# Weight-block loads of the projection jobs, and the stores of their split halves, issued from ScalarE's DMA queue instead of SyncE's

## The chip, the cores and the metric

One core of one Trainium2 chip runs the whole program. The metric is device time in microseconds (us), the median of several executions.

## What is computed

One layer of a streaming encoder over 2048 prompt rows and 32 sample rows of width 1024, all in float32. What matters here, from the reference:

```
z = h @ w_in                                  # 1024 x 10256: q, k, v, gates, ...
o, s_new = gated_delta_chunked(q, k, v, ...)  # per head, 64-frame blocks, a serial state S
merged = sigmoid(..) * (y_a @ w_proj_a) + sigmoid(..) * (y_b @ w_proj_b)
h1 = layer_norm(ALPHA * h + merged @ w_out, ...)
ple = sigmoid(h1 @ w_ple_gate) * (p @ w_ple)
h2 = layer_norm(ALPHA * h1 + ple, ...)
```

Every large product is made in three passes: each matrix is split into a rounded high part and a low part (the rest), and high*high, high*low and low*high are added up.

## The kernel before

The rows are worked in two halves (`HALVES`): half 0 has 1024 prompt rows and the 32 sample rows, half 1 the other 1024 prompt rows. A half goes through three stages: the projection jobs of `w_in` ("wz", 80 blocks of 128 output columns) with the gated delta rule woven in between; the merge (`merge`), jobs with the branch matrices "wb" and "wa" (8 blocks each) and the last gates of "wz"; and the row stages `out_rows` and `ple_rows` (through `rows`), with "wo" and "wg", whose pieces are the moving operand.

**A weight block.** `load_w` (L229) brings one block of 128 x 1024 into two tiles, `wh` (high) and `wl` (low), which have two buffers each. In half 0 a block is met for the first time: the raw block is loaded into `wr` (two buffers, L247), ScalarE rounds it into `wh` (L248), VectorE (or GpSimd, in the row stages) subtracts to get `wl` (L249), and both parts are stored to DRAM (L251) for later. When the same block is needed again, its two parts are loaded directly (L243). All of these transfers, and every other one of the kernel, are issued by SyncE (SP, "SPq" in the rows).

**Jobs.** A `Job` (L254) is one weight block times all columns of the half: 3 groups of 352 columns in half 0, 2 groups of 512 in half 1, 24 matmuls per group (L273), then an evacuation of the accumulator by ScalarE or VectorE. `run` (L280) calls `load` for the next job before it writes out the groups of the current one. Between the matmuls `fill.pump()` takes steps of the delta rule: its preparation (`delta_prep`, with small transfers at L600, L641, L645, L656, L659) and its state loop (`delta_loop`, L758 to L786), which pass through TensorE, VectorE and ScalarE in turn.

**Row stages.** `rows` (L979) loads a piece (L998, L1004) and multiplies it with the row tiles (L988 to L991). `out_rows` loads `lnx` tiles (L1043) and stores them (L1055), `ple_rows` loads them and `pw` tiles (L1064, L1081).

**Order.** The program is written in one sequence; the tile framework orders the instructions of each engine by priority, among those whose inputs and buffers it expects to be there. On the chip each engine and each queue takes its own instructions in that fixed order.

Of the kernel before, what the change touches and what calls it, by code (L numbers as in the profile page):

```python
# [8 lines left out]
F32 = mybir.dt.float32  # L9
# [84 lines left out]
def hybrid_kernel(ctx: ExitStack, tc: tile.TileContext, I, O):  # L94
    nc = tc.nc
    ve, ac, po, pe = nc.vector, nc.scalar, nc.gpsimd, nc.tensor
# [129 lines left out]
                ac.copy(out=oh, in_=p[:, :, :n])  # L226
                ve.tensor_tensor(out=lo[:, 4 * b:4 * b + 4, l0:l0 + n], in0=p[:, :, :n], in1=oh.bitcast(F32), op=ALU.subtract)

    def load_w(name, at, low, into=None):  # L229


        src, kept = I[name], split_d[name]
        for i in at:
            src, kept = src[i], kept[i]

        def cut(x):
            return x.rearrange("p (a b) -> p a b", a=2) if into else x

        parts = into or [wp.tile([128, 1024], F32R, tag=x, name=x) for x in ("wh", "wl")]
        hi, lo = parts  # L240
        if (name, at) in stored:
            for i, t in enumerate(parts):
                nc.sync.dma_start(out=t.bitcast(F32), in_=cut(kept[i]))  # L243
            return parts
        stored.add((name, at))
        raw = cut(wp.tile([128, HP + NS], F32, tag="wr", name="wr")[:, :1024])
        nc.sync.dma_start(out=raw, in_=cut(src))  # L247
        ac.copy(out=hi, in_=raw)  # L248
        low.tensor_tensor(out=lo, in0=raw, in1=hi.bitcast(F32), op=ALU.subtract)  # L249
        for i, t in enumerate(parts):  # L250
            nc.sync.dma_start(out=cut(kept[i]), in_=t.bitcast(F32))  # L251
        return parts

    class Job:  # L254
# [6 lines left out]

        def load(self):
            if self.w is None:
                self.w = load_w(self.src[0], self.src[1:], ve)

        def group(self, g0, n):
            rh, rl = self.x or (xh, xl)
# [12 lines left out]
    def run(jobs, first=0, back=False, between=None):  # L280


        with tc.high_priority(1500):
            for j in jobs[:first]:
                if j.open:
                    j.open()
                j.load()
        for i, g in enumerate(jobs[0].groups[::-1] if back else jobs[0].groups):
            for j in jobs[:first]:
                j.group(*g)  # L290
            if i == 0 and between:
                between()
        for j in jobs[:first]:
            if j.close:
                j.close()
        jobs = jobs[first:]
        for i, j in enumerate(jobs):
            if j.open:
                j.open()
            j.load()  # L300
            if i + 1 < len(jobs):
                jobs[i + 1].load()
            for g in j.groups:
                j.group(*g)
            if j.close:
                j.close()


    def phase0(hf, lp, g, b, batches):
# [83 lines left out]
    def beta_decay(hf, gp):  # L393
# [90 lines left out]

        job = Job(None, hf.groups, None, close)
        job.load, job.group = load, group
        return job, out

# [420 lines left out]
    def merge(hf, mp):  # L909
# [54 lines left out]
        for c in range(KT):  # L964
            wa[c].open = lambda c=c: load_gate(c)
        run(gb_ + wb + late + wa)
        for g in hf.ogroups:
            for k in range(KT):
# [6 lines left out]
    def hold(q):  # L975

        load_w("wg", (1, q), po, [t[:, 2 * q:2 * q + 2, 512:HP] for t in (xh, xl)])

    def rows(src, npiece, kh, kl, cols, done, after=None, last=1):  # L979
# [17 lines left out]
        for q in range(npiece - last):  # L997
            w = load_w(*src(q), po)  # L998
            for kk in range(2):
                for a, (t0, n) in zip(accs, cols):  # L1000
                    step(a, t0, n, 2 * q + kk, *w, halves[kk])
            if after:
                after(q)
# [132 lines left out]
    for hf in HALVES:  # L1136
        with pool(f"gp{hf.idx}") as gp:
# [15 lines left out]
            for h in range(H + hf.sample):  # L1153
                cols = Cols(sc[h == H], slice(0, 8) if h == H else slice(8 * h, 8 * h + 8))
                u, t, g = Us[h % 2], ts[h], smp_got if h == H else got[h]
# [10 lines left out]
            jobs += bj + [gate_a_job(hf, c, gp) for c in range(KT)]  # L1166
            fill.rate = [0.275, 0.56] if hf.sample else [0.41, 0.82]
            run(jobs, 3, *((True, lambda: deque(reload, 0)) if hf.idx else ()))
            fill.drain()
        early.close()  # L1170
# [103 lines left out]
```

## Time and profile before

| | us |
|---|---|
| median of 3 runs | 3216.71 (3216.45 to 3217.76) |
| the profiled execution, its own time | 3223.0 |
| its span, first to last instruction | 3221.3 |
| TensorE (PE) busy | 3065.1 (95%) |
| VectorE (DVE) busy | 1911.1 (59%) |
| ScalarE (ACT) busy | 887.2 (28%) |

Busy times are sums over one execution. DMA-issuing instructions are not counted as busy, so ScalarE's and SyncE's shares do not hold what a transfer costs its issuer. A wait line names who waited, for whom, the sum in us, the number of waits and the longest.

### The profile page before, as it was taken

To read this page: it belongs to the slowest core of one execution; us is meant where nothing else is said; L and a number is where in the kernel's file an instruction comes from. 1 tells how busy PE (TensorE), PEld (TensorE's weight loads), DVE (VectorE), ACT (ScalarE), POOL (GpSimd) and SP (SyncE) were. 2 spreads that over 40 slices of the span, in tenths; PEclk is the share of its full clock that TensorE was granted. 3 is DMA by queue.
4 is the path that set the end of the run, shared out by engine and by line. 5 is a ranking of instruction groups with operands and counts; after the bars stand their busy time and mean duration, and the time that the engine had idled before them with its cause. 6 is when DMAs were issued, how large, how long until landed. Compare 5 with 4: busy or idle time off the path is not lost.

```text
span 3221.3 us, 51399 instructions
## 1 busy us (share of the span) xinstructions
PE 3065.1 (95%) x20524; PEld 2679.5 (83%) x20524; DVE 1911.1 (59%) x4759; ACT 887.2 (28%) x2152; POOL 225.4 (7%) x349
## 2 busy tenths in 40 slices
PE   7999999999999999999989999999999999999997
PEld 5998899999999999997767877778877788888776
DVE  6866887777877422343656568777677730123366
ACT  3333443343333221221212223333233211111010
POOL 2110000100000000002221000000000000000001
PEclk8999999999999999999989999999999999999999
DMA  7643233333333454557773322232322234444685
GB/s 281 230 151 110 91 125 115 122 121 119 117 110 121 150 199 166 181 187 256 277 259 131 119 90 84 82 96 84 96 90 85 84 110 145 158 131 133 227 299 189
DMA packets 176416, 477.07 MB, mean 148 GB/s; under 512 B 54640, under 2 KB 59280, under 8 KB 175792
## 3 DMA queue, kind: packets, MB, share of 16 engines
q1 hardware_dynamic: 176176, 473.78, 42.7%
q8 instruction: 161, 2.64, 0.3%
q14 instruction: 79, 0.65, 0.1%
HBM read 293.29 MB, written 180.41 MB: 147 GB/s over the span
## 4 chain that ended last, share of the span: by engine, by line
PE 68%; DVE 18%; issue 8%; DMA 3%; POOL 1%; ACT 1%; SPq 0%; DVEq 0%; POOLq 0%; ACTq 0%
PE acc L273 56%; DVE ktm L559 4%; DVE vtm L559 3%; DVE at L559 1%; DVE v L523 1%; PE oo L768 1%; PE sc L777 1%; PE oo L778 1%; PE sc L766 1%; POOL sg L1088 1%; PE sc L758 1%; DVE dt L609 1%; PE pp L686 1%; PE pp L629 1%; DVE lnx L206 1%
## 5 line engine op out<-in xcount | busy, mean ns | idle before, releaser
L273 PE MATMUL acc<-xh,wl 128*128 128x352 f32 (+1 forms) x3200 | 718.0, 361 | 0.0
L273 PE MATMUL acc<-xh,wh 128*128 128x352 f32 (+1 forms) x3200 | 714.5, 359 | 0.7 <-ACT xh L226 0.7
L273 PE MATMUL acc<-xl,wh 128*128 128x352 f32 (+1 forms) x3200 | 711.3, 359 | 0.0
L273 PEld LDWEIGHTS acc<-xh,wl 128*128 128x128 f32 x3200 | 553.7, 190 | 54.4 <-issue 1.6
L273 PEld LDWEIGHTS acc<-xh,wh 128*128 128x128 f32 x3200 | 552.0, 190 | 55.3 <-issue 1.4
L273 PEld LDWEIGHTS acc<-xl,wh 128*128 128x128 f32 x3200 | 551.6, 190 | 53.1 <-issue 1.8
L248 ACT CAST wh<-wr 128x1024 fp32r<-128x1024 f32 x112 | 117.3, 1048 | 266.3 <-PE acc L273 197.8
L249 DVE TENSOR_TENSOR wl<-wr,wh 128x1024 fp32r<-128x1024 f32 x96 | 117.2, 1221 | 73.6 <-PE acc L273 43.7
L919 DVE TENSOR_TENSOR yl<-yr,yh 128x1056 fp32r<-128x1056 f32 (+1 forms) x32 | 39.7, 1241 | 164.1 <-DMA ga_d<-ga 90.8
L273 PE MATMUL acc<-yh,wl 128*128 128x352 f32 (+1 forms) x640 | 133.9, 351 | 0.0
L273 PE MATMUL acc<-yl,wh 128*128 128x352 f32 (+1 forms) x640 | 133.9, 351 | 0.0
L273 PE MATMUL acc<-yh,wh 128*128 128x352 f32 (+1 forms) x640 | 133.9, 351 | 0.0
L273 PEld LDWEIGHTS acc<-yh,wh 128*128 128x128 f32 x640 | 111.5, 188 | 10.9
L273 PEld LDWEIGHTS acc<-yl,wh 128*128 128x128 f32 x640 | 111.5, 188 | 10.8
L273 PEld LDWEIGHTS acc<-yh,wl 128*128 128x128 f32 x640 | 111.5, 188 | 10.8
L559 DVE STREAM_TRANSPOSE at<-q 32x256 f32<-32x256 f32 x256 | 111.6, 436 | 11.2 <-PE pp L726 7.3
L559 DVE STREAM_TRANSPOSE ktm<-vtm 32x256 f32<-32x256 f32 x260 | 113.2, 435 | 4.0
L559 DVE STREAM_TRANSPOSE vtm<-v 32x256 f32<-32x256 f32 x256 | 111.5, 436 | 6.7 <-ACT v L524 2.5
L559 DVE STREAM_TRANSPOSE ktm<-k 32x256 f32<-32x256 f32 x256 | 111.5, 436 | 6.3 <-ACT k L524 2.2
L780 DVE SCALAR_TENSOR_TENSOR S<-S,gl,sc 128x128 f32<-128x128 f32 x136 | 46.7, 344 | 104.7 <-PE sc L777 103.2
L508 ACT COPY z<-acc 128x352 f32<-128x352 f32 (+3 forms) x144 | 61.8, 446 | 169.1 <-PE acc L273 168.8
L774 ACT ACTIVATE v<-sc,bk 128x128 f32<-128x128 f32 (+1 forms) x136 | 49.4, 363 | 207.8 <-DVE v L772 207.4
(320 smaller groups left out, 4461.3 us busy)
## 6 DMA issues: line engine op xcount, KB each, us to landing
wr<-wz SPq DMA_DIRECT2D x80, 512.0 KB, 4.4
wz_d<-wh SPq DMA_DIRECT2D x80, 512.0 KB, 2.6
wz_d<-wl SPq DMA_DIRECT2D x80, 512.0 KB, 2.9
wl<-wz_d SPq DMA_DIRECT2D x80, 512.0 KB, 4.1
wh<-wz_d SPq DMA_DIRECT2D x80, 512.0 KB, 3.4
lnx<-h_d SPq DMA_DIRECT2D x40, 512.0 KB, 5.8
h_d<-lnx SPq DMA_DIRECT2D x32, 512.0 KB, 3.1
wh<-wo_d SPq DMA_DIRECT2D x24, 512.0 KB, 4.5
```

What stands on the lines that cost most here:

```text
L206: ve.scalar_tensor_tensor(out=x[:n], in0=x[:n], scalar=mv[:n, i, 0:1], in1=g[:n], op0=ALU.subtract, op1=ALU.mult)
L248: ac.copy(out=hi, in_=raw)
L249: low.tensor_tensor(out=lo, in0=raw, in1=hi.bitcast(F32), op=ALU.subtract)
L273: pe.matmul(out=a[:, :n], lhsT=wt[:, k * 128:(k + 1) * 128], rhs=xt[:, k, g0:g0 + n], start=i == 0, stop=i == 23)
L508: ac.copy(out=t["z"][:, c0:c0 + m], in_=a[:, o:o + m])
L523: ve.scalar_tensor_tensor(out=a[:, :L], in0=z[:, i:i + L], scalar=wca[:, cb, i:i + 1], in1=a[:, :L], op0=ALU.mult, op1=ALU.add)
L559: ve.transpose(out=dst[b:b + 32, :, a:a + 32], in_=src[a:a + 32, :, b:b + 32])
L609: ve.tensor_tensor_scan(out=d, data0=ones[:P, :P], data1=d, initial=0.0, op0=ALU.mult, op1=ALU.add)
L629: pe.matmul(out=p[:, c, :], lhsT=k[:, 4 * b + c, :], rhs=k[:, 4 * b + c, :], start=True, stop=True)
L774: ac.activation(out=v1, in_=pt, func=AF.Copy, scale=bk[:, col])
L780: ve.scalar_tensor_tensor(out=Sc, in0=Sc, scalar=sc["gl"][:, col], in1=pd, op0=ALU.mult, op1=ALU.add)
L919: ve.tensor_tensor(out=yl[:, k, :hf.nt], in0=raw, in1=yh[:, k, :hf.nt].bitcast(F32), op=ALU.subtract)
```

## The change

`load_w` gets a parameter `queue`. `Job.load` passes ScalarE, so the raw blocks and the stored parts of "wz", "wa" and "wb" are loaded from ScalarE's queue. The pieces of "wo" and "wg" in the row stages keep SyncE for their loads. The stores of all split parts go to ScalarE's queue; they are written into the program not behind the split but at the start of the next `load_w`, and at the end of `run`.

```diff
+    later = []
+
+    def store_split():
+
+        while later:
+            t, d = later.pop(0)
+            ac.dma_start(out=d, in_=t.bitcast(F32))
+
-    def load_w(name, at, low, into=None):
+    def load_w(name, at, low, into=None, queue=nc.sync):
...
         hi, lo = parts
+        store_split()
         if (name, at) in stored:
             for i, t in enumerate(parts):
-                nc.sync.dma_start(out=t.bitcast(F32), in_=cut(kept[i]))
+                queue.dma_start(out=t.bitcast(F32), in_=cut(kept[i]))
             return parts
         stored.add((name, at))
         raw = cut(wp.tile([128, HP + NS], F32, tag="wr", name="wr")[:, :1024])
-        nc.sync.dma_start(out=raw, in_=cut(src))
+        queue.dma_start(out=raw, in_=cut(src))
         ac.copy(out=hi, in_=raw)
         low.tensor_tensor(out=lo, in0=raw, in1=hi.bitcast(F32), op=ALU.subtract)
-        for i, t in enumerate(parts):
-            nc.sync.dma_start(out=cut(kept[i]), in_=t.bitcast(F32))
+        later.extend((t, cut(kept[i])) for i, t in enumerate(parts))
         return parts
...
-                self.w = load_w(self.src[0], self.src[1:], ve)
+                self.w = load_w(self.src[0], self.src[1:], ve, queue=ac)
...
             if j.close:
                 j.close()
+        store_split()
```

## Rows read from the trace of the kernel before

**Rows 1.** The head of the profile page: the span, and the busy time of each engine with its share of the span and its instructions.

```profile
span 3221.3 us, 51399 instructions
PE 3065.1 (95%) x20524; PEld 2679.5 (83%) x20524; DVE 1911.1 (59%) x4759; ACT 887.2 (28%) x2152; POOL 225.4 (7%) x349
```

**Rows 2.** Busy time by stretch of the span: start:end, length, then busy us (and instructions) of PE, PEld, DVE, ACT and POOL, the granted TensorE clock, the DMA share and GB/s. In order: the start, the delta rule of half 0, the row stages of half 0, the delta rule of half 1, the row stages of half 1.

```profile
0.00:80.00 80.00, 56.47 (x225) 43.00 (x226) 53.15 (x116) 30.98 (x49) 19.94 (x22) 0.85 0.76 282
...
240.00:1040.00 800.00, 756.51 (x6937) 730.54 (x6936) 616.64 (x1601) 311.30 (x869) 57.17 (x144) 0.98 0.33 116
...
1440.00:1760.00 320.00, 287.20 (x1285) 224.52 (x1284) 172.36 (x445) 63.94 (x97) 70.87 (x47) 0.94 0.66 235
1840.00:2560.00 720.00, 693.87 (x5503) 564.32 (x5502) 535.58 (x1429) 232.37 (x682) 28.24 (x69) 0.98 0.28 88
...
2960.00:3221.00 261.00, 231.02 (x1004) 184.95 (x1002) 133.34 (x365) 23.92 (x40) 17.90 (x12) 0.95 0.65 230
```

**Rows 3.** The waits of PE: tile and line, what released it, us in total, times, the longest.

```profile
PE pp L693 <- DVE M L676: 20.1, 9, 3.6
...
PE pp L675 <- POOL xs L646: 6.1, 1, 6.1
...
PE sc L988 <- ACT wh L248: 4.8, 2, 2.8
...
PE oo L988 <- ACT wh L248: 3.6, 1, 3.6
...
PE sc L989 <- POOL wl L249: 2.2, 2, 1.2
...
PE oo L989 <- POOL wl L249: 1.2, 1, 1.2
...
PE acc L273 <- ACT xh L226: 0.7, 1, 0.7
...
PE oo L778 <- ACT v L774: 0.3, 1, 0.3
```

**Rows 4.** The waits of SyncE's DMA queue, in the same form.

```profile
SPq L243 <- PE acc L273: 727.2, 151, 23.2
SPq L251 <- ACT wh L248: 552.0, 80, 17.4
SPq L251 <- DVE wl L249: 121.7, 59, 10.0
...
SPq L251 <- POOL wl L249: 23.0, 11, 2.3
```

**Rows 5.** What one issue takes on SyncE: the views of the three lines that issue weight transfers, count and min/median/max in ns, first and last start in us.

```profile
L251 SPq DMA_DIRECT2D wz_d<-wh x80: 319/320/1403, 25.7 to 1350.2; - x80
...
L247 SPq DMA_DIRECT2D wr<-wz x80: 332/424/2053, 16.7 to 1344.5; - x80
...
L243 SPq DMA_DIRECT2D wl<-wz_d x80: 319/320/424, 1707.7 to 2888.7; - x80
```

**Rows 6.** SyncE in order of time at three places of the row stages of half 0: start us, length us, queue, line, transfer, count.

```profile
1469.83 0.33 SPq L251 DMA_DIRECT2D wo_d<-wh  x1
1472.31 0.32 SPq L251 DMA_DIRECT2D wo_d<-wl  x1
1473.03 1.71 SPq L247 DMA_DIRECT2D wr<-wo  x2
...
1596.91 0.32 SPq L1055 DMA_DIRECT2D h_d<-lnx  x1
...
1597.80 0.73 SPq L251 DMA_DIRECT2D wg_d<-wl  x1
1598.59 0.49 SPq L247 DMA_DIRECT2D wr<-wg  x1
...
1622.42 0.42 SPq L251 DMA_DIRECT2D wg_d<-wl  x1
1622.89 2.19 SPq L247 DMA_DIRECT2D wr<-wg  x2
```

**Rows 7.** Busy time by stretch, as in Rows 2, for 20 us of the row stages of half 0.

```profile
1600.00:1610.00 10.00, 6.04 (x25) 3.88 (x23) 2.17 (x3) 4.46 (x6) 5.76 (x5) 0.84 0.94 361
1610.00:1620.00 10.00, 9.95 (x50) 8.16 (x51) 5.17 (x9) 3.94 (x8) 4.04 (x2) 0.82 0.45 143
```

**Rows 8.** All engines in order of time around two blocks in the delta rule of half 0: start us, length us, engine, line, operation, count, and in brackets the idle time before it and its releaser.

```profile
405.09 1.05 ACT L248 CAST wh<-wr 128x1024 fp32r<-128x1024 f32 x1 [2.07 <-PE acc L273]
...
419.04 1.05 ACT L248 CAST wh<-wr 128x1024 fp32r<-128x1024 f32 x1 [0.28 <-PE acc L273]
...
420.41 0.47 ACT L876 ACTIVATE cu<-acc 128x352 f32<-128x352 f32 x1 [0.32 <-PE acc L273]
...
426.01 1.22 DVE L249 TENSOR_TENSOR wl<-wr,wh 128x1024 fp32r<-128x1024 f32 x1
...
428.01 0.37 SPq L251 DMA_DIRECT2D wz_d<-wl  x1
...
428.43 0.43 SPq L247 DMA_DIRECT2D wr<-wz  x1
```

**Rows 9.** Waits of DVE for ACT, in the form of Rows 3.

```profile
DVE qs L735 <- ACT lj L583: 23.1, 10, 3.8
...
DVE vtm L785 <- ACT vtm L784: 20.9, 57, 1.8
```

## The prediction

> **What bounds the kernel now.** I read the page's head first, then the stretches, then who waits for whom, for PE and for SyncE's queue, and last the order of time where PE waits for a weight. PE is busy 3065.1 of 3221.3 us [rows 1], so 156 us of idle time is all that a change of queues can win back, apart from clock. The stretches say where it lies [rows 2]: 23.5 us at the start, 43.5 and 26.1 us in the two delta stretches, 32.8 and 30.0 us in the two row stages.
>
> The waits of PE say what it waits for [rows 3]. In the jobs (line 273) it waits 0.7 us in the whole run, and that for `xh`: no job ever waits for its weight block. In the delta stretches its largest sum is for VectorE (20.1 us at line 693). For split weight blocks it waits in one place only, the row stages of half 0: 4.8 + 3.6 us for the high part and 2.2 + 1.2 us for the low part, 11.8 us together.
>
> The queue that the change relieves, SyncE's, stands still much of the time [rows 4]: 727.2 us for PE to let go of a `wh` or `wl` buffer, 552.0 us for ScalarE's rounding, 121.7 and 23.0 us for the subtraction. Rows 8 show one such wait: the rounding ends at 420.09, VectorE makes the low part only at 426.01 to 427.23, the store goes out at 428.01, and the next raw load, which stood behind it, at 428.43. So a long wait in this queue is common, and the question is only who needs what stands behind it.
>
> **The change, part by part.**
>
> (1) *Issues moved.* From SyncE to ScalarE go 80 + 8 + 8 = 96 raw loads, 2 x (80 + 8 + 8 + 8 + 8) = 224 stores and 2 x 96 = 192 loads of stored parts: 512 issues. On SyncE a store or a stored-part load takes 0.320 us and a raw load 0.424 us [rows 5], so 192 x 0.32 + 224 x 0.32 + 96 x 0.42 = 173 us. No row shows an issue on ScalarE. The low bound is 0 (the engine could go on with what it holds), the high bound the longest raw issue of SyncE, 2.05 us. I take SyncE's medians, the nearest rows. ScalarE goes from 887 to 1060 us of 3221, which leaves it two thirds idle: it does not become the bound. What counts is what stands behind an issue.
>
> (2) *What an issue holds up on ScalarE.* A first-time block puts 2 x 0.32 + 0.42 = 1.06 us on ScalarE per job, and jobs follow each other at 419.04 - 405.09 = 13.95 us [rows 8]: 7.6% of the time. Evacuations behind it have three accumulators and a group of several us as cover. Without cover are the steps of the delta rule that go VectorE, ScalarE, VectorE; the two largest such sums have 10 + 57 = 67 waits, 23.1 + 20.9 us [rows 9]. If 7.6% of them meet a full 1.06 us, that is 67 x 0.076 x 1.06 = 5.4 us on VectorE. VectorE is busy 616.6 of 800 us there [rows 2], and PE waits for it only in part, so I take half, **+2.7 us**. Bounds: nothing, if all falls into ScalarE's slack (PE itself waits 0.3 us for `v` in the whole run [rows 3]); and 5.4 us and more if an issue also brings a wait, which is the rival below.
>
> (3) *Stores that wait on ScalarE.* The store of the low part needs VectorE's subtraction. The edit writes it one job later, but the order of issue is not that of the program: the rounding at 419.04 comes before the evacuation at 420.41 [rows 8], though the program has it behind that job's last evacuation. So a store may well go out as soon as its input is expected, and the postponement only gives way to other work that is ready. Priced at 0 here; the case where it isn't is the rival.
>
> (4) *Row stages of half 0.* Loads of "wo" and "wg" stay on SyncE; their stores leave it. At three places a raw load that PE later waits for stood directly behind such a store [rows 6]. At 1473.03 the queue had been free from 1470.16 but for the wait of the store at 1472.31: 2.9 us earlier. At 1598.59 the store took 0.73 us, and what holds the queue otherwise, the store of `lnx` at 1596.91, stays: 0.7 us. At 1622.89: 0.4 us. Together **-4.0 us** if the whole advance reaches PE. Bounds: 0, if the transfers and not the issue set the landing (the DMA engines were 94% busy in the 10 us from 1600 [rows 7]); and all 11.8 us. With them could go what the clock takes after the idle time: 0.84 and 0.82 granted, between 1.2 and 2.4 GHz, over 6.0 and 10.0 us of work, 0.16 x 6.0 + 0.18 x 10.0 = 2.8 us [rows 7].
>
> The Trainium skill, page "DMA: Bandwidth & Descriptors", section "Issuing engines are not separate DMA queues", says that transfers started by different engines share the same 16 DMA engines and that a second issuer saves only the issuing time. By that rule part (4) would save nothing, as 0.4 us per issue isn't on PE's path, and the sum would be +2.7 us. By rows 6 the first place saves a wait of the queue, not an issue, so I keep the 4.0 us.
>
> (5) *Jobs and the small transfers.* A block that is loaded later than now must still come before its job: a load issued when the buffer is free has a job of 13.95 us as cover [rows 8], and PE's 0.7 us shows no shortage [rows 3]. The small transfers of the preparation are no longer behind weight stores. PE waited 6.1 us for that chain once (line 675); its other waits there follow VectorE [rows 3]. Taken as 0, with 6.1 us as the far end.
>
> **Sum:** -4.0 + 2.7 = -1.3 us. The profiled execution (3223.0 us, span 3221.3) was 6.3 us above the median of the runs; the difference is taken off the median, 3216.7 - 1.3 = **3215.4 us**. Besides, any move gives the planner a new order on every engine. PE's waits at line 693 are 20.1 us in 9 waits of up to 3.6 us, out of 16 heads; a new draw of these alone can be several us away, either way. A change under 0.2% (6.4 us) cannot be told from none here.
>
> **Rivals.**
>
> *Faster: the queue held more than it seems.* If all 11.8 us of row-stage waits go, the 2.8 us of clock with them, and the 6.1 us of the first head, the time is 3216.7 - 20.7 = 3196.0 us. For it: the queue stands 552.0 and 727.2 us [rows 4]. Against: what stood behind it was nearly always early enough [rows 3]. Chance 0.31.
>
> *Slower: ScalarE stands where SyncE stood.* A store of a low part on ScalarE waits for VectorE, and the copies and squarings of the delta rule stand behind it. SyncE waited 121.7 us in 59 such waits [rows 4], each 2.1 us. If a fifth of that reaches PE through VectorE, it costs 24.3 us, and with part (4) the time is 3216.7 + 24.3 - 4.0 = 3237.0 us. It decides from about a twelfth on: 10.4 us of 121.7 make up for the 4.0 us and pass the 6.4 us. For it: in rows 8 the low part came 5.9 us after the rounding had ended. Against: ScalarE is idle for 61% of the delta stretch of half 0 [rows 2], and the delta step behind the wait mostly needs VectorE as well, in its order. The Trainium skill, page "Perfetto Trace Analysis", section "Per-instruction lifecycle", calls ScalarE's queue strictly first in, first out, which is this rival's condition; no row shows a transfer in that queue. Chance 0.25.
>
> *The postponement does nothing.* If stores go out as soon as their inputs are there, the edit is only a change of queue. That is part (3) as priced, inside the forecast.
>
> **How the numbers follow.** No change that can be told: 0.44; faster 0.31, slower 0.25. Within 0.2% is 3210.3 to 3223.1. The range takes in most of both rivals, down to 3200 (a full row-stage gain of 14.6 us and a little of the rest) and up to 3232 (two thirds of the slower rival's price).
>
> **What would show it.** Right: the lines 243, 247 and 251 on ScalarE's queue at some 0.3 to 0.4 us each; SyncE's waits for `wh` and `wl` gone but for "wo" and "wg" loads; PE's waits for `wh` and `wl` in the row stages of half 0 down by about a third; the delta stretches within 5 us of 43.5 and 26.1 us idle. Wrong: PE waits for ScalarE (`v`, `LL`) of more than a few us, or VectorE's waits for ScalarE clearly above those of rows 9; a first-time block's raw load landing so late that line 273 waits; an issue on ScalarE far from 0.4 us.

## The result and the profile after

| | before | after |
|---|---|---|
| median of 5 runs, us | 3216.62 (3214.38 to 3217.76) | 3250.86 (3248.50 to 3252.80) |
| span of the profiled execution, us | 3221.3 | 3249.8 |

The ratio is 1.010, with a 95% interval from 1.0088 to 1.0112: slower by 34 us, beyond the upper end of the range. The two profiled executions, from which the rest is read, stand 28.5 us apart: that of the kernel before was 6.3 us above its median. In the changed kernel the stores are L235, the loads of stored parts L252, the raw load L256, rounding and subtraction L257 and L258, the matmuls of the jobs L281, and the small transfers of the delta preparation L650, L654, L665 and L668.

The head of its page and its list of queues (packets, MB, share of the 16 DMA engines' time):

```profile
span 3249.8 us, 51328 instructions
...
PE 3075.5 (95%) x20524; PEld 2691.5 (83%) x20524; DVE 1911.0 (59%) x4759; ACT 881.4 (27%) x2152; POOL 217.9 (7%) x349
...
q10 hardware_dynamic: 73728, 268.47, 23.1%
q1 hardware_dynamic: 102448, 205.31, 18.5%
```

q10 is the new one: 268 MB of weights now travel beside q1, SyncE's. TensorE's work is 10 us longer than in [rows 1] with as many instructions, so part of the loss is clock, and the rest is idle time.

**Where.** A marker that means the same work in every kernel is the first matmul of the branch jobs (`acc<-yh,wh`): everything of half 0's delta rule lies ahead of it. It starts at 1241.1 us before and at 1272.6 after, so that stretch lost 31.5 us. From the first raw load of "wo" to the first load of "wz" in half 1, which is the row stages of half 0, it is 278.1 us before (1430.0 to 1708.1) and 267.9 after (1460.7 to 1728.6): 10.2 us won. From there to the last of these branch matmuls in half 1 it is 1287.2 us before (its start is 2995.3) and 1297.0 after (3025.6): 9.8 us lost again. The end is 28.5 us later. The stretch from the start to the marker, first before, then after, with the columns of [rows 2]:

```profile
0.00:1241.10 1241.10, 1174.08 (x9376) 1116.80 (x9377) 862.17 (x2155) 453.34 (x1131) 103.40 (x210) 0.98 0.41 146
...
0.00:1272.60 1272.60, 1187.85 (x9376) 1129.47 (x9377) 860.80 (x2155) 448.72 (x1131) 96.88 (x210) 0.96 0.39 142
```

With as many matmuls, TensorE is idle 17.7 us longer (84.7 for 67.0) and busy 13.8 us longer at a granted clock of 0.96 for 0.98. These two are the whole 31.5 us. The stretches of [rows 2] after, in the same order without the start and the end:

```profile
240.00:1040.00 800.00, 741.14 (x6701) 714.68 (x6701) 597.91 (x1524) 298.70 (x835) 51.57 (x142) 0.95 0.31 112
1440.00:1760.00 320.00, 291.96 (x1382) 236.87 (x1381) 174.46 (x450) 60.59 (x95) 69.65 (x45) 0.97 0.69 246
1840.00:2560.00 720.00, 690.02 (x5222) 561.95 (x5221) 520.86 (x1393) 230.80 (x673) 31.80 (x73) 0.98 0.28 90
```

In the first of them TensorE idles 58.9 us instead of 43.5: 15.4 us more. And its mean matmul takes 741.14 / 6701 = 0.1106 us instead of 756.51 / 6937 = 0.1091, at a granted clock of 0.95 instead of 0.98: 6701 x 0.0015 = 10 us more. So 25 of the 31.5 us fall into this stretch.

**What it waits for.** Of the waits of PE, first those that grew, then those that [rows 3] named in the row stages:

```profile
PE pp L684 <- DMA L<-l_d: 16.7, 11, 4.5
...
PE pp L735 <- DVE dt L697: 11.0, 4, 4.2
...
PE sc L786 <- DVE v L781: 9.4, 7, 2.8
...
PE acc L281 <- ACT ct L859: 2.5, 1, 2.5
PE sc L998 <- POOL wl L258: 2.0, 1, 2.0
...
PE acc L281 <- ACT z L517: 1.4, 1, 1.4
...
PE sc L997 <- ACT wh L257: 1.1, 1, 1.1
```

and of DVE, where the last two answer to [rows 9]:

```profile
DVE U L679 <- DMA L<-l_d: 31.5, 10, 8.0
...
DVE tm L661 <- DMA as<-a_d: 19.9, 11, 4.9
DVE vtm L794 <- ACT vtm L793: 19.4, 46, 1.6
...
DVE qs L744 <- ACT lj L592: 10.2, 7, 2.8
```

In the row stages the waits for split parts fell by more than forecast, from 11.8 us to 3.1. ScalarE did not slow VectorE: 19.4 and 10.2 us where 20.9 and 23.1 stood. What is new are waits for `as` and `L`, the small transfers of 8 and 64 KB by which the preparation of a chunk passes a matrix through DRAM. The same waits in the kernel before were short, for PE and for DVE:

```profile
PE pp L675 <- DMA L<-l_d: 1.4, 2, 0.7
...
DVE U L670 <- DMA L<-l_d: 6.6, 5, 3.4
...
DVE tm L652 <- DMA as<-a_d: 2.9, 4, 1.5
```

The transfers themselves land later. Here are four rows of the DMA issues before (bytes of each, then the median us from issue to landing):

```profile
a_d<-at SPq DMA_DIRECT2D x130, 8.0 KB, 1.5
L<-l_d SPq DMA_DIRECT2D x130, 8.0 KB, 1.7
...
as<-a_d SPq DMA_DIRECT2D x16, 64.0 KB, 3.1
l_d<-xs SPq DMA_DIRECT2D x16, 64.0 KB, 1.9
```

and after:

```profile
a_d<-at SPq DMA_DIRECT2D x130, 8.0 KB, 2.6
L<-l_d SPq DMA_DIRECT2D x130, 8.0 KB, 1.7
...
as<-a_d SPq DMA_DIRECT2D x16, 64.0 KB, 2.1
l_d<-xs SPq DMA_DIRECT2D x16, 64.0 KB, 3.6
```

The two writes to DRAM, `a_d` and `l_d`, take 1.1 and 1.7 us longer, and the reads behind them are issued when they have landed. (The read of `as` is shorter after: 2.3 us for 2.8 from 240 to 1040 us, and 2.1 for 4.4 from 1700 to 2800 us, in half 1. So the read wins back a part of what the write `a_d` loses, and in half 1 more than that; the read of `L` wins back nothing.) One place of the changed kernel, all engines in order of time, shows the whole step:

```profile
438.20 0.33 ACTq L235 DMA_DIRECT2D wz_d<-wl  x1
...
438.60 0.46 SPq L665 DMA_DIRECT2D l_d<-xs  x1
438.62 0.39 ACTq L256 DMA_DIRECT2D wr<-wz  x1
...
442.87 3.62 SPq L668 DMA_DIRECT2D L<-l_d  x8
...
444.40 0.29 PE L684 MATMUL pp<-L,at 32*32 32x16 f32 x2 [4.54 <-DMA L<-l_d]
```

`l_d` leaves between a 512 KB store and a 512 KB load of the other queue. The loads of `L`, which wait for it, follow 4.27 us later, and PE stands 4.54 us. The same work in the kernel before:

```profile
422.36 0.46 SPq L656 DMA_DIRECT2D l_d<-xs  x1
...
424.28 3.63 SPq L659 DMA_DIRECT2D L<-l_d  x8
```

There `L` follows 1.92 us after `l_d`. The weight load of [rows 8] came only at 428.43: in the same queue it stood behind these and behind the store that waited for the low part.

I take this to be the other side of the waits of [rows 4]. While SyncE's queue stood for ScalarE's rounding and for buffers, the weights behind were held with it. After, most of them run in the other queue, and SyncE's waits for the two small writes grew. Before:

```profile
SPq L659 <- DMA l_d<-xs: 29.6, 16, 3.5
...
SPq L645 <- DMA a_d<-at: 5.2, 11, 1.0
```

and after:

```profile
SPq L668 <- DMA l_d<-xs: 46.3, 17, 3.8
...
SPq L654 <- DMA a_d<-at: 39.5, 27, 3.7
```

### The profile page after: what moved, and what is told of

Its sections match the earlier page's. It is cut to its first block, busy times and chain, and to the rows that moved or that the text cites. A ratio compares the mean times of both kernels' runs of the same rounds, so it can differ in the third digit from the quotient of the medians.

```text
span 3249.8 us, 51328 instructions
## 1 busy us (share of the span) xinstructions
PE 3075.5 (95%) x20524; PEld 2691.5 (83%) x20524; DVE 1911.0 (59%) x4759; ACT 881.4 (27%) x2152; POOL 217.9 (7%) x349
## 3 DMA queue, kind: packets, MB, share of 16 engines
q10 hardware_dynamic: 73728, 268.47, 23.1%
q1 hardware_dynamic: 102448, 205.31, 18.5%
## 4 chain that ended last, share of the span: by engine, by line
PE 66%; DVE 18%; issue 7%; DMA 5%; POOL 1%; ACT 1%; SPq 1%; DVEq 0%; ACTq 0%; POOLq 0%
PE acc L281 54%; DVE ktm L568 4%; DVE vtm L568 2%; DVE v L532 1%; POOL sg L1097 1%; PE sc L786 1%; DVE at L568 1%; PE oo L777 1%; PE oo L787 1%; DVE lnx L206 1%; DMA L<-l_d 1%; PE pp L695 1%; PE sc L775 1%; PE sc L767 1%; DVE xs L662 1%
## 5 line engine op out<-in xcount | busy, mean ns | idle before, releaser
L281 PE MATMUL acc<-xl,wh 128*128 128x352 f32 (+1 forms) x3200 | 723.3, 362 | 0.0
L281 PE MATMUL acc<-xh,wh 128*128 128x352 f32 (+1 forms) x3200 | 716.9, 360 | 3.9 <-ACT ct L859 2.5
L281 PE MATMUL acc<-xh,wl 128*128 128x352 f32 (+1 forms) x3200 | 719.5, 361 | 0.0
L281 PEld LDWEIGHTS acc<-xl,wh 128*128 128x128 f32 x3200 | 557.7, 192 | 53.6 <-issue 1.8
L281 PEld LDWEIGHTS acc<-xh,wl 128*128 128x128 f32 x3200 | 556.2, 191 | 54.3 <-issue 1.6
L281 PEld LDWEIGHTS acc<-xh,wh 128*128 128x128 f32 x3200 | 552.6, 190 | 57.9 <-ACT ct L859 2.8
L257 ACT CAST wh<-wr 128x1024 fp32r<-128x1024 f32 x112 | 117.3, 1048 | 276.6 <-PE acc L281 188.9
L258 DVE TENSOR_TENSOR wl<-wr,wh 128x1024 fp32r<-128x1024 f32 x96 | 117.8, 1228 | 75.9 <-ACT wh L257 40.4
L281 PE MATMUL acc<-yl,wh 128*128 128x352 f32 (+1 forms) x640 | 133.9, 351 | 0.0
L281 PE MATMUL acc<-yh,wl 128*128 128x352 f32 (+1 forms) x640 | 133.9, 351 | 0.0
L281 PE MATMUL acc<-yh,wh 128*128 128x352 f32 (+1 forms) x640 | 133.9, 351 | 0.0
L281 PEld LDWEIGHTS acc<-yh,wh 128*128 128x128 f32 x640 | 111.5, 188 | 10.9
L281 PEld LDWEIGHTS acc<-yl,wh 128*128 128x128 f32 x640 | 111.5, 188 | 10.8
L281 PEld LDWEIGHTS acc<-yh,wl 128*128 128x128 f32 x640 | 111.5, 188 | 10.8
```

Of the source, the lines that this page charges most:

```text
L281: pe.matmul(out=a[:, :n], lhsT=wt[:, k * 128:(k + 1) * 128], rhs=xt[:, k, g0:g0 + n], start=i == 0, stop=i == 23)
```

## The experiments

Three theories. **A**: weight transfers in a second queue share the DMA engines with the small transfers of the delta preparation, these land later, TensorE and VectorE wait, and the clock falls with TensorE's idle time. **B**: ScalarE is held by stores that wait for VectorE, and the delta steps stand behind it (the slower rival of the prediction). **C**: the planner drew a worse order, whatever the queue. Beside each time stands the marker of the profiled run: the first branch matmul against 1241.1 us before. The kernel before ran beside each group, at 3217.4, 3219.3 and 3219.5 us; most of its single runs lie within some 9 us of that, so the ratios carry the verdicts. The marker is read from one execution of each kernel. In the six runs below that leave the weights of half 0's delta rule on SyncE and add no bulk, it lies from -4.4 to +7.8, so a difference of that size tells nothing by itself.

**The change in halves.** Loads of the three matrices on ScalarE, stores at once on SyncE (against the changed kernel):

```diff
-        later.extend((t, cut(kept[i])) for i, t in enumerate(parts))
+        for i, t in enumerate(parts):
+            nc.sync.dma_start(out=cut(kept[i]), in_=t.bitcast(F32))
```

> Half of the change: the jobs' raw blocks and stored parts are loaded from ScalarE's queue, the split parts are stored from SyncE's queue right behind the split, as in the kernel before. Theory A (weight transfers in a queue of their own run beside the small transfers of the delta preparation, which land later; TensorE waits for them and its clock falls): a third of the bytes of a half-0 job move, all of them in half 1; half 0 loses a third of its 31 us, half 1 its 8 us, the row stages gain nothing: about 3235 us. Theory B (ScalarE is held by stores that wait for VectorE): no such store is left on ScalarE, half 0 is as before, at most 8 us in half 1: 3217 to 3225 us. Theory C (the planner drew a worse order, the queue as such costs nothing): anything from 3205 to 3250 us, with the small transfers landing as before.

Measured: 3240.92 us, ratio 1.0070 (1.0051 to 1.0089), marker +1.9. The total is nearer to A's number (3235) than to B's, but the place is not A's: half 0, which was to lose a third of its 31 us, lost nothing that can be told, and the last branch matmul is 16.2 us later.

Stores postponed on ScalarE, loads on SyncE:

```diff
-                self.w = load_w(self.src[0], self.src[1:], ve, queue=ac)
+                self.w = load_w(self.src[0], self.src[1:], ve)
```

> The other half of the change: stores of split parts from ScalarE's queue with the next load, all loads from SyncE's queue as in the kernel before. A: two thirds of half 0's loss, about +21 us, nothing in half 1, the 9.5 us of the row stages won: about 3228 us. B: the whole of half 0's loss, +31 - 9.5: about 3238 us. C: anything, small transfers landing as before (medians near 1.5 us for the diagonal blocks, 1.9 us for the solved ones).

Measured: 3231.01 us, ratio 1.0039 (1.0026 to 1.0053), marker +16.7. That is nearer to A's numbers (+21, 3228) than to B's (+31, 3238). The two halves add up to the whole, 0.70 + 0.39% against 1.0%. In half 0 they seem not to, 1.9 + 16.7 against 31.5, as if loads cost there only together with the stores; no run tests that.

Everything on SyncE, the stores only postponed (`store_split` with SyncE, loads as before):

```diff
-            ac.dma_start(out=d, in_=t.bitcast(F32))
+            nc.sync.dma_start(out=d, in_=t.bitcast(F32))
```

> Only the postponement: the stores are written with the next load, but every transfer stays on SyncE's queue. A and B: no transfer runs beside another queue's and ScalarE issues nothing: 3217 us, within 6 us. C: the order is drawn anew here too, so a difference of over 10 us either way would speak for it.

Measured: 3219.66 us, ratio 1.0010 (0.9996 to 1.0024), marker +0.9. The postponement and the new order it brings cost nothing that can be told. Nothing here speaks for C.

Only the stores of "wo" and "wg", in the row stages, postponed on ScalarE:

```diff
+        if name in ("wo", "wg"):
+            later.extend((t, cut(kept[i])) for i, t in enumerate(parts))
+        else:
+            for i, t in enumerate(parts):
+                nc.sync.dma_start(out=cut(kept[i]), in_=t.bitcast(F32))
...
-                self.w = load_w(self.src[0], self.src[1:], ve, queue=ac)
+                self.w = load_w(self.src[0], self.src[1:], ve)
```

> Only the stores of the output-stage pieces (w_out and w_ple_gate, 32 stores of half 0's row stages) go to ScalarE's queue with the next load; all else as in the kernel before. A and B: the delta stretches are as before, the row stages of half 0 win what they won in the changed kernel, 9.5 us: about 3207 us. C: the gain need not come back; 3205 to 3225 us.

Measured: 3214.10 us, ratio 0.9983 (0.9970 to 0.9995), marker -1.6; the row stages of half 0 take 267.8 us (1428.5 to 1696.3) instead of 278.1. So the 10 us are these stores' and separable. In the median of the runs they show as 3 to 6.

**B by itself.** The kernel before, and ScalarE holds as in the change, with stores of 8 KB:

```diff
+    def hold_act():
+
+        while later:
+            t = later.pop(0)
+            d = dp.tile([128, 16], F32, tag="hold_d", name="hold_d", bufs=8)
+            ac.dma_start(out=d, in_=t[:, :16].bitcast(F32))
...
+        hold_act()
...
+        later.extend(parts)
```

> The kernel before, with all weight transfers on SyncE as they were, and added: ScalarE issues, with the next load and at a run's end, two stores of 8 KB from the split parts to a scratch tensor, which wait for the same casts and subtractions as the postponed stores of the change. ScalarE is held as in the change, in as many places, and nothing is moved. A: 3217 within 6. B (ScalarE stands at stores that wait for VectorE, and the delta steps behind it): the loss of the run with the postponed stores alone, 3228 to 3236, the first wb store 15 us later.

Measured: 3213.36 us, ratio 0.9985 (0.9975 to 0.9996), marker -1.4. ScalarE was held: with work behind it, it waited for VectorE's low part 29.7 us in seven waits, where the change has 19.8 us in four. It cost nothing, and B falls.

**A by itself, at first badly aimed.** The kernel before, and GpSimd copies 512 KB with each load of "wz"; beside it the same with 8 KB:

```diff
+    def beside(at):
+
+        t = dp.tile([128, 1024], F32, tag="extra_d", name="extra_d", bufs=4)
+        po.dma_start(out=t, in_=I["wz"][at])
...
+                if self.src[0] == "wz":
+                    beside(self.src[1])
```

> The kernel before, with one thing added: with each load of a wz block GpSimd issues a copy of 512 KB of that block to a scratch tensor that nothing reads. SyncE keeps all of its transfers in their order, ScalarE issues nothing. A (bulk traffic in a second queue makes the small transfers of the delta steps land late, and TensorE and VectorE wait for them): l_d<-xs from 1.9 us towards 2.5 us or more, TensorE at pp behind L<-l_d above the 1.4 us of before, the first wb store 10 to 25 us later, time 3227 to 3250. B (only ScalarE's being held costs): no change, 3217 within 6. A third reading, that GpSimd's own issuing costs, would show in the tiny copies beside this run as well.

> As the run with the copies of 512 KB, with the same number of copies from GpSimd, but of 8 KB each. A: no traffic to speak of, 3217 within 6, landings as before. If GpSimd's issuing is what costs, this run is as slow as the one with the large copies.

Measured: 3356.99 us, ratio 1.0424 (1.0408 to 1.0440), against 3213.24 us, 0.9982 (0.9970 to 0.9993). The bytes cost, the issuing does not. But the large loss is not the one looked for: nothing made GpSimd wait, so all 160 copies were issued by 426.7 us and filled the DMA engines. Of the run with the large copies, two stretches:

```profile
0.00:400.00 400.00, 242.05 (x1500) 219.64 (x1501) 189.07 (x457) 90.18 (x167) 115.49 (x215) 0.80 0.88 321
400.00:1040.00 640.00, 607.66 (x5496) 585.59 (x5495) 497.52 (x1263) 254.61 (x696) 56.89 (x137) 0.98 0.37 132
```

TensorE is busy 242 of the first 400 us at a DMA share of 0.88; the marker is 139.7 us later, and the last branch matmul 133.7: nothing is lost after the flood. The landings go with it: from 240 to 430 us the median `a_d` took 25.9 us, from 430 to 1040 us 1.5. So bytes in a second queue can hold up the small writes, but here by filling the DMA engines, which the change does not do.

**A with the bytes taken out.** The pair that decides most. Of each "wz" block but the first, half 0 moves 64 of 1024 columns, once in the kernel before and once in the changed one (here the former):

```diff
-        nc.sync.dma_start(out=raw, in_=cut(src))
...
+        few = lambda x: x if whole else x[:, :64]
+        nc.sync.dma_start(out=few(raw), in_=few(cut(src)))
+        full = few(raw)
...
+        if not whole:
+            full = full.unsqueeze(1).to_broadcast([128, 16, 64])
+            h3, l3 = [t.rearrange("p (a b) -> p a b", a=16) for t in parts]
+        ac.copy(out=h3, in_=full)
...
-            nc.sync.dma_start(out=cut(kept[i]), in_=t.bitcast(F32))
+            nc.sync.dma_start(out=few(cut(kept[i])), in_=few(t.bitcast(F32)))
```

> The kernel before with the bytes of wz cut in half 0: of each block but the first, 64 of 1024 columns are loaded, the cast and the subtraction read them 16 times over (as many elements as before), and 64 columns of each split part are stored; half 1 loads the first block's parts for every block, in full. Left out: the other columns of wz. It is the measure for the run beside it and should itself be 0 to 15 us faster than before, since waits for transfers are small there (L<-l_d 1.4 us, wh and wl of wz under 5): 3202 to 3217.

> The changed kernel with the same cut of wz in half 0: every issue, wait and place on ScalarE's queue is the change's, only the bytes of half 0 are a sixteenth. Left out: the other columns of wz. A (the bytes in the second queue delay the small transfers): the loss of the delta stretch of half 0 goes away, first wb load within 6 us of the run beside it, its time 0 to 10 us above that run's (half 1 keeps its 8, the row stages give 9 back). B (ScalarE held, or another order of the work): the loss stays, first wb load 25 to 31 us later, the time 25 to 35 above.

Measured: before with the cut 3218.55 us, ratio 1.0002 (0.9987 to 1.0016), marker +0.5; after with the cut 3215.66 us, ratio 0.9996 (0.9986 to 1.0006), marker -7.6. In the kernel before the bytes of half 0 cost nothing that can be told. In the changed one they go with the whole loss: with as many issues on the same queues, the marker goes from +31.5 to -7.6. (A expected the first "wb" load within 6 us of the run beside it and the time 0 to 10 us above; the load is 8.1 us earlier and the time 2.9 us below.) The changed kernel with the cut, in the stretch of the delta rule of half 0:

```profile
240.00:1040.00 800.00, 758.59 (x6979) 733.14 (x6980) 619.07 (x1592) 312.76 (x872) 57.23 (x145) 0.99 0.09 23
```

41.4 us idle instead of 58.9, at a clock of 0.99 instead of 0.95. Its landings from 240 to 1040 us:

```profile
a_d<-at SPq DMA_DIRECT2D x58, 8.0 KB, 1.5
l_d<-xs SPq DMA_DIRECT2D x8, 64.0 KB, 1.9
```

are those of before again. From 240 to 1060 us VectorE's wait for `as<-a_d` goes from 14.3 to 0.8 us and that for `L<-l_d` from 16.7 to 7.0. B, which this run leaves in place (ScalarE waits for VectorE's low part 15.4 us in four waits), has no part of the loss in half 0. C is not shut out by the pair alone. The cut changes the planner's order too: of the 1341 instructions and issues of ScalarE ahead of the marker, 1074 stand in the same order in both runs. In half 1, where both move the blocks in full, the loss stays: from the first "wz" load to the first "wb" load it is 1077.3 us (1690.7 to 2768.0) against 1065.3 in the run beside it (1708.8 to 2774.1), 12 us. There the same run's small writes are late again (1700 to 2800 us):

```profile
a_d<-at SPq DMA_DIRECT2D x64, 8.0 KB, 2.4
l_d<-xs SPq DMA_DIRECT2D x8, 64.0 KB, 2.9
```

The landings by half, from the same two stretches of each run, speak against C. Medians in us of `a_d` and `l_d`:

| run | full weight blocks in ScalarE's queue | half 0 | half 1 |
|---|---|---|---|
| kernel before | none | 1.5, 2.1 | 1.5, 1.9 |
| changed kernel | half 0 loads and stores, half 1 loads | 2.7, 3.6 | 2.5, 3.6 |
| loads alone | half 0 loads, half 1 loads | 1.5, 2.8 | 2.6, 3.1 |
| stores alone | half 0 stores | 1.7, 3.6 | 1.5, 1.9 |
| changed kernel with the cut | half 1 loads | 1.5, 1.9 | 2.4, 2.9 |

In the other runs that leave the weights of these stretches on SyncE and add no bulk, `a_d` takes 1.5 us throughout and `l_d` 1.9 to 2.8. So in four kernels with different orders the small writes are clearly late only where full blocks run in the other queue, though the raw loads alone did little in half 0. C expected the landings as before. Whether the new order takes a share of the 39 us, of the size of the marker's scatter, stays open.

**Bytes added in other places.** ScalarE stores `wh` of "wz" a second time, to scratch, right after its own rounding:

```diff
         ac.copy(out=hi, in_=raw)
+        if name == "wz":
+            again(hi)
...
```

> The kernel before, SyncE unchanged, and ScalarE stores each wz block's wh a second time, 512 KB to a scratch tensor, right after its own cast, so without waiting for another engine. 80 transfers, 42 MB beside SyncE's, spread over half 0 as the blocks are. If bytes beside the small transfers cost by themselves: L and as land later, and the first wb load comes 8 to 20 us later, 3225 to 3240. If what cost in the change is that SyncE no longer holds the weights back while it waits for the small chain, or if ScalarE's being held is what costs: 3217 within 6.

Measured: 3232.08 us, ratio 1.0049 (1.0028 to 1.0070), marker +6.7. The time and the first "wb" load, 10.6 us later (1222.4 before, 1233.0 here), lie within what was expected if bytes cost by themselves. The added stores run in half 0 alone; there, from 240 to 1040 us:

```profile
l_d<-xs SPq DMA_DIRECT2D x8, 64.0 KB, 3.2
as<-a_d SPq DMA_DIRECT2D x7, 64.0 KB, 3.2
```

for 2.1 and 2.8 us in the kernel before and at most 2.8 in the runs without bulk; `a_d` keeps its 1.5. So 42 MB more in the second queue made two of the four small transfers somewhat later, on seven or eight of each. The marker's 6.7 us lie within its scatter. And the store of `wh` moved there instead of doubled:

```diff
         ac.copy(out=hi, in_=raw)
+        if name == "wz":
+            ac.dma_start(out=kept[0], in_=hi.bitcast(F32))
...
+            if i or name != "wz":
```

> The kernel before with one store moved: wh of each wz block is stored from ScalarE's queue right after the cast that ScalarE did itself, wl and the loads stay on SyncE. No bytes are added, ScalarE waits for nobody. Bytes beside the small transfers: 5 to 15 us later at the first wb load, 3222 to 3232. B: 3217 within 6. A gain of up to 5 us is possible too, since SyncE has one wait for a cast less in front of the small transfers.

Measured: 3223.29 us, ratio 1.0012 (1.0000 to 1.0024), marker +2.2. Here the first "wb" load is 2.3 us later, not 5 to 15, and 42 MB moved left the small transfers where they were (1.5, 1.9 and 2.2 us for `a_d`, `l_d` and `as` in that stretch). So bytes in a second queue are not enough; where they run counts too. I read it so: right after the rounding SyncE is about to store the same block, and its order keeps the small chain behind or ahead of that moment; in the change nothing does. No run takes away that order alone, so this is argued and not shown.

**A version from it.** ScalarE's queue only where no delta step runs: the jobs of the merge, loads and postponed stores, and the stores of the row stages.

```diff
+        for j in gb_ + wb + late + wa:
+            j.merge = True
         run(gb_ + wb + late + wa)
```

> The change only where no delta step runs: loads and postponed stores on ScalarE for the jobs of the merge, postponed stores on ScalarE for the blocks of the row stages; the jobs of the delta stretches keep SyncE with their stores at once. A: the gain of the row stages without the loss, 3208 to 3215, the first wb store within 2 us of before, the first wz load of half 1 about 11 us earlier. B: the same in the row stages, up to 5 us more in the merge if ScalarE's stores stand there behind VectorE's subtractions: 3209 to 3219.

Measured: 3212.69 us, ratio 0.9976 (0.9965 to 0.9986), marker +7.8; row stages of half 0 269.2 us (1437.0 to 1706.2). The loss of the whole change is gone. It is not shown to be a gain: the two runs that add only tiny transfers stand at 0.9982 and 0.9985, with intervals that overlap this one, so some 0.15% is within what any edit moves here. Two of the marks set for it were missed: the first "wb" store is 9.2 us later, not within 2, and the first load of "wz" in half 1 is 1.9 us earlier, not 11. The marker's 7.8 us are no cost of the moved transfers: the first of them leaves at 1155.0 us, and at 936 us the same matmul of the jobs already starts 7.1 us later than before.

## Why the prediction was wrong

The step that failed is **(5)**, "The small transfers of the preparation are no longer behind weight stores", "Taken as 0, with 6.1 us as the far end". It saw only the queue's order, and only a gain: what stood behind a weight store would leave earlier. That they would then run beside weights was not priced, although [rows 4] gave the hint: SyncE stood for 727.2 and 552.0 us, with the weights behind it. Its far end should have been a loss, and no sign of being wrong named the small transfers. The runs showed in its place that `a_d` and `l_d` land 1.1 and 1.7 us later. The pair with the cut bytes measures the term: from +31.5 to -7.6 us at the end of half 0's delta rule, 39 us, with a scatter of some 8, and some 12 more in half 1. The sign for being right, delta stretches within 5 us of 43.5 and 26.1 us idle, failed in half 0 (58.9) and held in half 1 (30.0).

(1) was right: stores and stored-part loads take 0.326 us on ScalarE and raw loads of "wz" 0.340 us in the median; forecast were 0.32 and 0.42:

```profile
L235 ACTq DMA_DIRECT2D wz_d<-wh x80: 326/326/377, 29.6 to 1381.6; - x80
...
L252 ACTq DMA_DIRECT2D wh<-wz_d x80: 326/326/358, 1728.6 to 2917.1; - x80
...
L256 ACTq DMA_DIRECT2D wr<-wz x80: 339/340/1686, 22.0 to 1375.9; - x80
```

(2), +2.7 us for delta steps behind ScalarE's issues: not seen. VectorE's waits for ScalarE fell, and the run that only holds ScalarE is no slower than before.

(3) was half right. ScalarE did stand for the subtraction with other work behind it, in four waits of the changed kernel's list, and PE met it twice, for 2.5 and 1.4 us (lines L281 above):

```profile
ACT cu L885 <- DVE wl L258: 6.1, 1, 6.1
...
ACT L910 <- DVE wl L258: 5.9, 1, 5.9
ACT za L548 <- DVE wl L258: 5.9, 1, 5.9
...
ACT z L440 <- DVE wl L258: 1.9, 1, 1.9
```

The first of them is not all the store's: before the same `cu` the kernel before shows a wait of 3.5 us for the low part too, with no transfer on ScalarE.

(4) was right in its side and too small: -4.0 forecast, 10.2 us measured on the row stages, within its own bound of 14.6. Of these, 6.1 us are idle time of TensorE (27.9 before, 21.8 after) and 4.1 busy time with as many matmuls, at a clock of 0.97 for 0.94. Four other runs with these stores off SyncE have 267.8 to 269.4 us there, seven that keep them on it 276.7 to 284.4 (the run with the large copies aside). Its largest place was misread. After the store at 1472.31 the raw load still waited 0.4 us, until 1473.01, for a transfer of `ln_out`, so without the store it could hardly have left 2.9 us earlier; what won the 6.1 us place by place was not followed up.

The slower rival had the side and not the mechanism: its condition, a queue in strict order, held in (3), its price did not. The sentence of the Trainium skill, page "DMA: Bandwidth & Descriptors", section "Issuing engines are not separate DMA queues", that transfers of different issuers interleave on the same 16 engines, was used in the prediction against a gain. The trace agrees with it (q1 and q10 share them, 18.5 and 23.1%). It could also have been read as a warning for (5): here the two small writes took 1.1 and 1.7 us more beside the 512 KB blocks. What the prediction drew from it, a saving of issuing time and nothing else, did not hold in this case: the row stages won 10.2 us, and the whole lost 34.

The result also passed the range because idle time was counted once. With 17.7 us more of it ahead of the marker the granted clock fell from 0.98 to 0.96 and the matmuls took 13.8 us longer. The forecast had such a pair in [rows 7] and used it for a gain of 2.8 us only. That the idle time is what lowered the clock fits both, and no run here tests it.

## What to carry to other kernels

A queue that stands in order can also be what keeps bulk transfers away from the small ones on the critical chain. Before bulk gets a queue of its own, list the small transfers that somebody waits for within a few us, their time to land and how often the chain passes through them. In the row stages, where no such chain runs, taking the stores off SyncE won some 10 us. To test it, keep every issue and cut only the bytes, and read the landings in the stretches where the bytes run: a median over the whole run mixes stretches with and without them, and hides what the doubled stores and the large copies did.

## What the runs showed of the hardware

A small write of 8 or 64 KB took 1.5 and 1.9 us to land, and 2.6 and 3.6 us with weights free to run in a second queue. The mean DMA share over half 0's delta stretch was only 0.31 there, and 0.33 before: the mean did not show it. An issue costs ScalarE about what it costs SyncE, 0.326 to 0.320 us. Stores of 42 MB added right behind ScalarE's rounding took `l_d` from 2.1 to 3.2 us in that stretch and left `a_d` at 1.5; as many bytes moved there, and not added, left both where they were. In the run with the large copies, with the DMA engines 88% busy over the first 400 us, the median `a_d` took 25.9 us from 240 to 430 us.
